# The 60 dependent steps that invert the 32 by 32 triangles: from VectorE to GpSimd

## The chip, the cores and the metric

One core of a Trainium2 chip runs the whole network. The time is device microseconds (us) of one execution. Engines are called as in the profile: PE is TensorE (matmuls), DVE is VectorE, ACT is ScalarE, POOL is GpSimd, SP issues the weight loads.

## The reference

Two layers on 256 frames of width 2048 in float32. Layer 0 mixes tokens by RWKV-7 (16 heads of 64) beside a Mamba-2 scan, layer 1 by chunked attention; each is followed by a SwiGLU feed-forward. What matters here is the RWKV-7 recurrence:

```
def step(S, inp):
    r_t, w_t, k_t, v_t, a_t, b_t = inp
    sa = jnp.einsum('bhvk,bhk->bhv', S, a_t)
    S = S * w_t[:, :, None, :] + sa[..., None] * b_t[:, :, None, :] + v_t[..., None] * k_t[:, :, None, :]
    return S, jnp.einsum('bhvk,bhk->bhv', S, r_t)
```

The kernel does it in four chunks of 64 frames. Within a chunk each step feeds on the ones before it, so that a unit triangular system of 64 rows is solved for each head: its inverse is built from two triangles of 32 rows on the diagonal and one block under them.

## The kernel before, in words

Every large product x W is a stream (`mm_chunk` and `stream`, lines 223 to 264): SP loads a weight tile, ACT makes its rounded part `hi` (line 240), DVE the rest `lo` (line 241, two inputs in SBUF), and PE multiplies hi and lo with both halves of the activations (lines 260 to 262). One weight tile of 128 by 512 makes six such matmuls of 512 columns, three for each half of the frames. `hi` and `lo` have five buffers each in layer 0's mixer, so DVE can be at most five tiles ahead of PE.

`mixer0` (line 393) handles the RWKV heads in two halves of eight (`rwkv_half`, line 481). A half projects k, r and v through the stream, and then:

- PE forms the products `aa` of all chunks and heads (line 576), and DVE masks them into `AA` (line 580).
- DVE transposes the two diagonal blocks of 32 chunk-head pairs into `NB` (line 589, two instructions).
- The forward substitution follows (lines 590 to 595): for i from 1 to 30 one multiplication writes `itmp`, and one addition puts it into the rows of `NB` that are left. Each of the 60 instructions reads what the one before it wrote. They work on 64 partitions and on (31 - i) x i elements of each, from 30 to 240; over i these are 4960 elements, so 9920 for both instructions.
- POOL sets the diagonal to one (line 596). DVE transposes the result into `Sf` (line 624, two instructions) and `TG` (line 625).
- PE needs `TG` for the 32 small matmuls `ga` (line 633), and `TG` and `Sf` for the 32 `gb` (line 640). With them the 64-row inverse is complete.
- The four chunks then go one after another (`cx`, `cu`, `ch`, `cy`, lines 651 to 717).

Beside this, PE runs `bo` (line 603) and the transpositions `bt` and `vt` (lines 612 and 616). After both halves comes the Mamba-2 part; for each of two groups it has transpositions `xt` (line 817), a mask `L` multiplied on POOL (line 826), cumulative sums `sg` (line 831), the exponential and a product on ACT and DVE, and `yd` (line 838).

The order in which instructions stand on each engine is set at build time by a scheduler that works with times of its own and with priorities: the stream has one raised by 4000, the rest of the mixer has none. On the chip every engine takes its instructions strictly in that order, so an instruction that waits holds up all that stand behind it on its engine. POOL otherwise has memsets (lines 596, 618, 621, 688), a few DMA issues and the four multiplications of line 826.

The line that the change touches is 146, and it acts on lines 593 and 595:

```
inv = dve
...
inv.tensor_tensor(tv, NB[:, i + 1:32, i:i + 1].broadcast_to([64, nt, i]),
                  NB[:, i:i + 1, 0:i].broadcast_to([64, nt, i]), op=ALU.mult)
inv.tensor_tensor(NB[:, i + 1:32, 0:i], NB[:, i + 1:32, 0:i], tv, op=ALU.add)
```

Of the kernel before, what the change touches and what calls it, by code (L numbers as in the profile page):

```python
# [142 lines left out]
def encoder_body(ctx: ExitStack, tc: tile.TileContext, A):  # L143
    nc = tc.nc
    act, dve, pool, pe = nc.scalar, nc.vector, nc.gpsimd, nc.tensor
    inv = dve

    cst = ctx.enter_context(tc.tile_pool(name="cst", bufs=1))
    wpool = ctx.enter_context(tc.tile_pool(name="wpool", bufs=5))
# [846 lines left out]
```

## Time and profile before

| | |
|---|---|
| median of three runs | 2382.67 us (2381.77 to 2384.16) |
| the profiled execution | 2384.66 us, its span 2382.8 us |
| busy in the span: PE, DVE, ACT, POOL | 2352.1, 1428.8, 1267.5, 32.4 us |
| mean granted PE clock | 0.992 |
| first chain of substitutions, on DVE | from 115.55 to 149.37 us |
| second chain | from 266.73 to 320.10 us |

Times in the trace count from the span's start. A matmul's end is modelled, so PE counts as busy in stretches where it is slow: what it gets done is seen from the distance between the starts of its matmuls, from its waits and from the granted clock (1.00 is 2.4 GHz, 0.50 is 1.2 GHz).

### The profile page before, as it was taken

Reading aid. Unit: us, or ns where it says so; the run is one execution under the profiler, and the core shown is the slowest. Engines: PE = TensorE matmul, PEld = TensorE weight load, DVE = VectorE, ACT = ScalarE, POOL = GpSimd, SP = SyncE. Lnnn points to the kernel's source line nnn. Section 1 sums busy time; section 2 is a strip of 40 time slices with the busy share of each in tenths; the row PEclk is TensorE's granted clock in tenths of the full one; section 3 lists DMA queues with packets and bytes.
Section 4 is the critical chain, followed back from the end, with each engine's and each line's share of the span. In section 5 each row is a group of like instructions: output and inputs, shape, how many; then the busy total and the mean of one; then the engine's idle time right before and its main releaser. Section 6 shows DMA issues by size and latency. Waiting matters only on the chain.

```text
span 2382.8 us, 31654 instructions
## 1 busy us (share of the span) xinstructions
PE 2352.1 (99%) x11426; PEld 1923.9 (81%) x11426; DVE 1428.8 (60%) x2380; ACT 1267.5 (53%) x2254; POOL 32.4 (1%) x61
## 2 busy tenths in 40 slices
PE   9999999999999999999999999999999999999998
PEld 7767777878888888888887888887888888888887
DVE  6876977765555555555557555557555555555554
ACT  6646545665545545544446555556555545454443
POOL 0000000000000000000000000000000000000000
PEclk9989999999999999999999999999999999999999
DMA  7434434666666666666665655565666666666664
GB/s 239 144 116 123 133 106 151 188 176 197 190 187 193 188 190 189 193 186 202 197 206 182 186 178 165 170 194 180 192 188 192 189 188 189 193 187 194 201 197 146
DMA packets 119357, 429.17 MB, mean 180 GB/s; under 512 B 13408, under 2 KB 13664, under 8 KB 119200
## 3 DMA queue, kind: packets, MB, share of 16 engines
q1 hardware_dynamic: 115280, 415.35, 57.2%
q0 software_dynamic: 2400, 9.18, 1.4%
q10 hardware_dynamic: 1520, 2.63, 0.4%
q8 instruction: 89, 1.46, 0.3%
q14 instruction: 68, 0.56, 0.1%
HBM read 425.01 MB, written 2.10 MB: 179 GB/s over the span
## 4 chain that ended last, share of the span: by engine, by line
PE 93%; DVE 4%; ACT 1%; DMA 1%; issue 1%; SPq 0%; DVEq 0%; ACTq 0%
PE mm_w_gu L260 13%; PE mm_w_gu L262 13%; PE mm_w_gu L261 13%; PE mm_w_dn L260 7%; PE mm_w_dn L262 7%; PE mm_w_dn L261 7%; PE mm_w_qkv L261 4%; PE mm_w_qkv L260 4%; PE mm_w_qkv L262 4%; PE mm_w_in L262 3%; PE mm_w_in L261 3%; PE mm_w_in L260 3%; PE mm_w_oab L260 1%; PE mm_w_oab L262 1%; PE mm_w_oc L262 1%; PE mm_w_oc L260 1%
## 5 line engine op out<-in xcount | busy, mean ns | idle before, releaser
L241 DVE TENSOR_TENSOR lo_w_gu<-raw_w_gu,hi_w_gu 128x512 fp32r<-128x512 f32 x704 | 485.8, 691 | 417.4 <-ACT hi_w_gu L240 414.9
L240 ACT CAST hi_w_gu<-raw_w_gu 128x512 fp32r<-128x512 f32 x704 | 438.4, 624 | 452.7 <-DVE lo_w_gu L241 404.9
L261 PE MATMUL mm_w_gu<-lo_w_gu,sh_f 128*128 128x512 f32 x1408 | 550.0, 391 | 0.0
L260 PE MATMUL mm_w_gu<-hi_w_gu,sh_f 128*128 128x512 f32 x1408 | 549.3, 390 | 0.6 <-ACT sh_f L299 0.5
L262 PE MATMUL mm_w_gu<-hi_w_gu,sl_f 128*128 128x512 f32 x1408 | 548.6, 390 | 0.0
L241 DVE TENSOR_TENSOR lo_w_dn<-raw_w_dn,hi_w_dn 128x512 fp32r<-128x512 f32 x352 | 242.8, 691 | 221.6 <-ACT hi_w_dn L240 221.0
L240 ACT CAST hi_w_dn<-raw_w_dn 128x512 fp32r<-128x512 f32 x352 | 219.0, 624 | 248.3 <-DVE lo_w_dn L241 238.6
L260 PEld LDWEIGHTS mm_w_gu<-hi_w_gu,sh_f 128*128 128x128 f32 x1408 | 264.3, 188 | 57.9 <-ACT sh_f L299 3.4
L262 PEld LDWEIGHTS mm_w_gu<-hi_w_gu,sl_f 128*128 128x128 f32 x1408 | 264.4, 188 | 55.5 <-DVE sl_f L300 1.2
L261 PEld LDWEIGHTS mm_w_gu<-lo_w_gu,sh_f 128*128 128x128 f32 x1408 | 264.4, 188 | 54.1 <-DVE lo_w_gu L241 0.3
L261 PE MATMUL mm_w_dn<-lo_w_dn,hh 128*128 128x512 f32 x704 | 274.1, 389 | 0.0
L262 PE MATMUL mm_w_dn<-hi_w_dn,hl 128*128 128x512 f32 x704 | 274.0, 389 | 0.0
L260 PE MATMUL mm_w_dn<-hi_w_dn,hh 128*128 128x512 f32 x704 | 273.9, 389 | 0.0
L241 DVE TENSOR_TENSOR lo_w_qkv<-raw_w_qkv,hi_w_qkv 128x512 fp32r<-128x512 f32 x192 | 132.2, 690 | 104.5 <-ACT hi_w_qkv L240 104.0
L240 ACT CAST hi_w_qkv<-raw_w_qkv 128x512 fp32r<-128x512 f32 x192 | 119.0, 621 | 110.3 <-DVE lo_w_qkv L241 64.8
L260 PE MATMUL mm_w_in<-hi_w_in,sh_in 128*128 128x512 f32 (+1 forms) x384 | 156.7, 408 | 1.7 <-ACT hi_w_in L240 1.7
L262 PE MATMUL mm_w_in<-hi_w_in,sl_in 128*128 128x512 f32 (+1 forms) x384 | 157.7, 411 | 0.0
L261 PE MATMUL mm_w_in<-lo_w_in,sh_in 128*128 128x512 f32 (+1 forms) x384 | 155.7, 405 | 0.0
L240 ACT CAST hi_w_in<-raw_w_in 128x512 fp32r<-128x512 f32 x184 | 112.3, 619 | 81.5 <-PE mm_w_in L262 71.5
L262 PEld LDWEIGHTS mm_w_dn<-hi_w_dn,hl 128*128 128x128 f32 x704 | 132.2, 188 | 27.6
L260 PEld LDWEIGHTS mm_w_dn<-hi_w_dn,hh 128*128 128x128 f32 x704 | 132.2, 188 | 27.3
L261 PEld LDWEIGHTS mm_w_dn<-lo_w_dn,hh 128*128 128x128 f32 x704 | 132.2, 188 | 27.2
(349 smaller groups left out, 2824.9 us busy)
## 6 DMA issues: line engine op xcount, KB each, us to landing
raw_w_gu<-in_w_gu SPq DMA_DIRECT2D x352, 512.0 KB, 3.6
raw_w_dn<-in_w_dn SPq DMA_DIRECT2D x176, 512.0 KB, 3.7
raw_w_qkv<-in_w_qkv SPq DMA_DIRECT2D x96, 512.0 KB, 3.6
raw_w_in<-in_w_in SPq DMA_DIRECT2D x92, 512.0 KB, 3.7
raw_w_oab<-in_w_oab SPq DMA_DIRECT2D x32, 512.0 KB, 4.2
raw_w_oc<-in_w_oc SPq DMA_DIRECT2D x32, 512.0 KB, 4.2
bias<-in_bias POOLq DMA_DIRECT2D x4, 768.0 KB, 6.6
x_in<-in_x SPq DMA_DIRECT2D x4, 512.0 KB, 9.0
```

The costliest lines, as they stand in the source:

```text
L240: act.copy(hi, raw[:, h, :])
L241: dve.tensor_tensor(lo, raw[:, h, :], hi.bitcast(F32), op=ALU.subtract)
L260: pe.matmul(o, lhsT=xh, rhs=h_[:, :width], start=k_ == 0, stop=False)
L261: pe.matmul(o, lhsT=xh, rhs=l_[:, :width], start=False, stop=False)
L262: pe.matmul(o, lhsT=xl, rhs=h_[:, :width], start=False, stop=k_ == nk - 1)
```

## The change

The 120 instructions of the two chains (60 in each half) are issued on POOL. All other lines stay as they are.

```
-    inv = dve
+    inv = pool
```

The scheduler builds another order from it. Three places matter; names end in buffer numbers, and "x2" means that the row is there twice in a row.

On POOL, where the first half's chain begins. Before:

```order
L598 DMA g_0_1255<-in_g 128x1024
L618 MEMSET uv_1266 64x512 x2
L618 MEMSET uv_1267 64x512 x2
L621 MEMSET Sf_1320 32x32x32
L596 MEMSET NB_986 64x32
```

With the change:

```order
L598 DMA g_0_1255<-in_g 128x1024
L593 ISA
L593 TENSOR_TENSOR itmp_988<-NB_986 64x30
L595 TENSOR_TENSOR NB_986<-NB_986,itmp_988 64x30
L593 TENSOR_TENSOR itmp_988<-NB_986 64x58
```

The chain stands ahead of the memsets of `uv` and `Sf`; in the second half four memsets of `uv` and the one of `Sf` stand within it. The row `ISA` stood ahead of line 826 before.

On DVE, what stands around the transpositions of the finished `NB` in the first half. Before:

```order
L595 TENSOR_TENSOR NB_986<-NB_986,itmp_988 64x30
L241 TENSOR_TENSOR lo_w_in_1_1_1956<-raw_w_in_1_1949,hi_w_in_1_1_1955 128x512
L624 STREAM_TRANSPOSE Sf_1320<-NB_986 32x32x32
L241 TENSOR_TENSOR lo_w_in_2_0_1974<-raw_w_in_2_1971,hi_w_in_2_0_1973 128x512
L624 STREAM_TRANSPOSE Sf_1320<-NB_986 32x32x32
L625 STREAM_TRANSPOSE TG_987<-NB_986 32x32x32
```

With the change:

```order
L604 TENSOR_TENSOR bv_1257<-bo_1258,bkv_468 128x512
L241 TENSOR_TENSOR lo_w_in_3_0_1733<-raw_w_in_3_1730,hi_w_in_3_0_1732 128x512
L604 TENSOR_TENSOR bv_1257<-bo_1261,bkv_468 128x512
L241 TENSOR_TENSOR lo_w_in_3_1_1737<-raw_w_in_3_1730,hi_w_in_3_1_1736 128x512
L625 STREAM_TRANSPOSE TG_987<-NB_986 32x32x32
L241 TENSOR_TENSOR lo_w_in_4_0_1755<-raw_w_in_4_1752,hi_w_in_4_0_1754 128x512
L624 STREAM_TRANSPOSE Sf_1320<-NB_986 32x32x32 x2
```

Between the second row of line 589 and the first of these transpositions stood 22 rows of line 241; now there are 10. In the second half there were 33 and are now 8; with the change line 624 comes first there, then two rows of line 241, line 624, one row of line 241, and line 625.

On PE, where the first half's `ga` stands among the stream. Before:

```order
L260 MATMUL mm_w_in_0_1925<-hi_w_in_1_0_1951,sh_in_122 128x512
L261 MATMUL mm_w_in_0_1925<-lo_w_in_1_0_1952,sh_in_122 128x512
L633 MATMUL ga_1325<-TG_987,AA_937 32x32 x32
L262 MATMUL mm_w_in_0_1925<-hi_w_in_1_0_1951,sl_in_123 128x512
```

With the change:

```order
L262 MATMUL mm_w_in_0_1662<-hi_w_in_2_0_1710,sl_in_125 128x512
L616 MATMUL vt_1313<-cc,bkv_468 128x128 x4
L633 MATMUL ga_1325<-TG_987,AA_937 32x32 x32
L260 MATMUL mm_w_in_1_1663<-hi_w_in_2_0_1710,sh_in_124 128x512
```

The stream matmuls (lines 260 to 262) counted in the whole order: from the last `aa` of the first half to its `ga` 160 before and 77 now; from there to the last `aa` of the second half 246 and 257; from there to the second half's `ga` 227 and 85. Eight transpositions of line 424 move behind `ga` in each half as well; those of the first half still stand ahead of the second half's `aa`. The first group's `xt`, `sg` and `yd` stood between the matmuls of the second half's four chunks; now they follow them, with runs of 7 and 9 stream matmuls between them.

## Rows read from the trace of the kernel before

**Rows 1.** The page: busy time by engine, and the chain that ended last.

```profile
PE 2352.1 (99%) x11426; PEld 1923.9 (81%) x11426; DVE 1428.8 (60%) x2380; ACT 1267.5 (53%) x2254; POOL 32.4 (1%) x61
...
PE 93%; DVE 4%; ACT 1%; DMA 1%; issue 1%; SPq 0%; DVEq 0%; ACTq 0%
```

**Rows 2.** Busy by stretch: us, PE, PEld, DVE, ACT, POOL; PE clock, DMA share, GB/s.

```profile
160.00:164.00 4.00, 4.00 (x69) 2.46 (x67) 0.69 (x1) 0.91 (x2) 0.00 (x0) 0.50 0.41 129
...
328.00:332.00 4.00, 4.00 (x73) 3.24 (x73) 2.86 (x5) 0.92 (x2) 0.00 (x0) 0.50 0.59 216
...
400.00:404.00 4.00, 3.13 (x14) 2.25 (x12) 1.65 (x3) 0.57 (x2) 0.00 (x0) 1.00 0.75 249
404.00:408.00 4.00, 1.59 (x8) 1.59 (x8) 3.56 (x5) 2.57 (x6) 0.00 (x0) 0.79 0.45 143
408.00:412.00 4.00, 4.00 (x13) 2.97 (x13) 0.84 (x2) 0.07 (x1) 1.83 (x1) 0.50 0.43 133
```

**Rows 3.** PE in order of time: start, us, work, [idle before it, what ended it].

```profile
121.06 0.82 PE L424 MATMUL tr<-cc,tm 128*128 128x128 f32 x6
134.28 0.63 PE L612 MATMUL bt<-cc,bkv 128*128 128x128 f32 x4 [1.71 <-DVE bv L604]
146.96 0.39 PE L260 MATMUL mm_w_in<-hi_w_in,sh_in 128*128 128x512 f32 x1
...
149.68 0.39 PE L260 MATMUL mm_w_in<-hi_w_in,sh_in 128*128 128x512 f32 x1
...
156.55 0.74 PE L633 MATMUL ga<-TG,AA 32*32 32x32 f32 x64 [2.44 <-DVE TG L625]
...
327.94 1.07 PE L633 MATMUL ga<-TG,AA 32*32 32x32 f32 x64 [3.93 <-DVE TG L625]
```

**Rows 4.** DVE in order of time: `NB` in the halves, and line 567.

```profile
98.94 1.67 DVE L567 SCALAR_TENSOR_TENSOR r<-r,pf,a 128x256 f32<-128x256 f32 x4
112.28 2.03 DVE L589 STREAM_TRANSPOSE NB<-AA 32x1024 f32<-32x1024 f32 x1
...
262.07 4.02 DVE L589 STREAM_TRANSPOSE NB<-AA 32x1024 f32<-32x1024 f32 x2
```

**Rows 5.** DVE groups by line and shape: busy us, mean ns of one.

```profile
L241 DVE TENSOR_TENSOR lo_w_in<-raw_w_in,hi_w_in 128x512 fp32r<-128x512 f32 x184 | 124.7, 687 | 35.1 <-ACT hi_w_in L240 34.3
L531 DVE TENSOR_TENSOR lw<-c,lw 128x1024 f32<-128x1024 f32 x2 | 2.4, 1222 | 0.0
L593 DVE TENSOR_TENSOR itmp<-NB 64x240 f32<-64x240 f32 x4 | 1.6, 391 | 0.0
L593 DVE TENSOR_TENSOR itmp<-NB 64x30 f32<-64x30 f32 x4 | 0.7, 184 | 0.0
```

**Rows 6.** POOL in order of time, from the start to line 826.

```profile
0.75 0.31 POOL L173 MEMSET warm<- 128x256 f32 x1 [0.29 <-POOLq L988]
...
15.17 0.18 POOL L193 COPY tick<-x_in 128x1 f32<-128x1 f32 x1 [12.81 <-DMA x_in<-in_x]
...
66.72 0.54 POOL L598 DMA_DIRECT2D g<-in_g  x1 [49.25 <-PE lo L520]
...
100.72 0.98 POOL L618 MEMSET uv<- 64x512 f32 x2 [8.37 <-DVE r L567]
...
275.67 0.94 POOL L621 MEMSET Sf<- 32x1024 f32 x1 [21.39 <-DVE NB L595]
316.28 0.15 POOL L596 MEMSET NB<- 64x32 f32 x1 [39.67 <-DVE NB L595]
316.45 2.14 POOL L826 TENSOR_TENSOR L<-cc,adt 128x1024 f32<-128x1024 f32 x1
334.15 1.90 POOL L826 TENSOR_TENSOR L<-cc,adt 128x1024 f32<-128x1024 f32 x1 [15.56 <-PE xt L817]
```

**Rows 7.** DVE in order of time, beside POOL's line 826.

```profile
316.75 1.91 DVE L593 TENSOR_TENSOR itmp<-NB 64x58 f32<-64x58 f32 x1
318.59 0.46 DVE L768 SCALAR_TENSOR_TENSOR xf<-tr_cv,hcv,xf 128x253 f32<-128x253 f32 x1
```

## The prediction

> **What bounds the kernel now.** I read the page first. PE is busy for 99% of the span and makes up 93% of the chain that ended last; POOL is almost idle [rows 1]. The stream therefore sets the time, and the change can only win where PE waits or runs slowly, and only lose by making PE wait. I looked next at PE in order of time for the two places where it needs the inverted triangles. Twelve stream matmuls start between 146.96 and 149.68, so one costs 0.227 us. PE then waits 2.44 us for `TG` before the first `ga`, at 156.55, and 3.93 us before the second, at 327.94 [rows 3]. By stretch, both waits are followed by some us at a granted clock of 0.50, half speed [rows 2]. That is all there is to win at these places: 6.4 us of waiting, and at least 2 us for each of the two stretches of 4 us at half clock.
>
> Last I looked at what hides the chain now. It shares DVE with the `lo` instructions, but PE has long work ahead of `ga`: 160 stream matmuls in the first half and 227 in the second, counted in the order of instructions. So a chain on DVE of 34 and 53 us costs PE almost nothing.
>
> **The chain itself.** On DVE one instruction takes 184 ns for 30 elements and 391 ns for 240 [rows 5]: 0.986 ns an element and 154 ns fixed. A half's 60 instructions with 9920 elements thus cost DVE 60 x 0.154 + 9.8 = 19.0 us, which DVE now saves twice. It gains PE nothing of its own where DVE waits for PE anyway.
>
> On POOL only line 826 is of this kind. It takes 1.90 us for 1024 elements undisturbed; a copy of one element takes 0.18 us [rows 6]. That gives 1.68 ns an element. The chain of a half then costs 60 x 0.18 = 10.8 us and 9920 x 1.68 ns = 16.7 us: 27.5 us.
>
> Each of the 60 instructions also needs the result of the one before. No row shows POOL waiting for itself. At the lower end the hand-over is free. The nearest row is POOL's start at 100.72 [rows 6], 0.11 us after line 567 ended on DVE at 98.94 + 1.67 = 100.61 [rows 4]. At the upper end I put 0.29 us, POOL's idle time ahead of `warm` [rows 6]. I take 0.11, since it is a wait for data on POOL: 6.6 us a half.
>
> DVE and POOL also get in each other's way. While line 826 ran on POOL from 316.45, a DVE instruction of line 593 with 58 elements and two inputs in SBUF took 1.91 us, and it ended with POOL's; the next on DVE, line 768, which reads PSUM and SBUF, had its usual length [rows 7]. The `lo` instructions of 687 ns [rows 5] have two inputs in SBUF, and 10 stand ahead of line 625 in the first half, 8 ahead of line 624 in the second. After that DVE itself waits for the chain and disturbs it no more. A `lo` costs the chain between nothing and 0.69 us; I take 0.4, somewhat over half: 4.0 and 3.2 us.
>
> The Trainium skill, SBUF — State Buffer, section "Who interferes with whom", says that a DVE instruction with two SBUF inputs and a GpSimd instruction that reads SBUF shut each other out for a whole instruction; the trace agrees, with the 1.91 us above.
>
> So the first chain takes T = 27.5 + 6.6 + 4.0 = 38.1 us. The second has five memsets among its instructions, four of `uv` (0.98 us for two) and one of `Sf` (0.94) [rows 6]: T' = 27.5 + 6.6 + 3.2 + 2.9 = 40.2 us. The row `ISA` is free: it stood between 316.28 + 0.15 and 316.45 before, and POOL now meets it after 67.3, long before the chain [rows 6].
>
> The Trainium skill, GPSIMD Engine Reference, section "Performance versus the Vector engine", speaks against the change: an addition of two inputs takes GpSimd 1.96 times as long as DVE. Line 531 on DVE takes 1.22 us for 1024 elements [rows 5], so the rows here give 1.56. By the page's ratio the 27.5 us would be an estimated 37.2, and the time below would come out near 2445.
>
> **What becomes late.** The scheduler has put `ga` where it believes the chain to be over: 77 stream matmuls after the last `aa` instead of 160, and 85 instead of 227. If the chain ends later, PE waits in front of `ga`, and DVE waits in front of line 625 or 624 with all `lo` behind it, so the stream can't fill the hole. In the first half PE could be at `ga` by about 135: the transpositions end at 121.9, 27 stream matmuls (6.1 us) and eight groups of `bt` and `vt` of 0.63 us [rows 3] make 133, and `bt` waits some 2 us for line 604. With `NB` ready at 114.3 [rows 4] a chain of over 20 us is late.
>
> The sum follows the two `ga`:
>
> - First `ga`: 114.3 + T + 2.0 (line 625; a transposition takes 2.03 [rows 4]) = 154.4 instead of 156.55: T - 40.2 = -2.1 us. PE arrives about as before but has done 83 stream matmuls less.
> - From there to the second half's `aa`: 257 stream matmuls instead of 246, and eight transpositions more (0.82 us for six [rows 3]): 2.5 + 1.1 = +3.6 us.
> - Second `ga`: `NB` is ready at 266.1 [rows 4]. Behind the chain come line 624 twice, line 625 and three `lo`, 8.2 us. Relative to `NB` this is T' + 8.2 instead of 61.8: T' - 53.6 = -13.4 us.
> - What is then still to do: 83 - 11 + 142 = 214 stream matmuls, 48.5 us, and eight transpositions, 1.1 us: +49.6 us.
>
> Together T + T' - 40.6 = 37.7 us. One term is left: the first Mamba group's `xt`, `sg` and `yd` were woven into the second half's chunks and now stand with short runs of stream, as the second group's do. There PE loses 0.87 + 2.41 us between 400 and 408, and about 2 us at half clock after that [rows 2]; with the 0.79 in between 5.6 us. Lower end nothing, upper end twice that with a longer half clock, 12 us. I take 5.6.
>
> The profiled execution took 2384.66 us. 2384.7 + 37.7 + 5.6 = 2428.0; the median of the runs lies 2.0 lower, so **2426 us**.
>
> **The rivals.**
>
> - *A dear hand-over.* At 0.29 us, and with every `lo` costing 0.69, T = 51.8 and T' = 53.3: +64.5, with 12 for the rest 2459 us. For it: 120 hand-overs in a row, whose price no row shows. Against: the 0.11 us.
> - *A short chain that is still late.* No hand-over, no mutual blocking: T = 27.5, T' = 30.4, +17.3 and nothing else: 2400 us. For it: POOL's memsets follow each other without a gap; against: those don't depend on each other.
> - *Faster: POOL keeps DVE's pace.* If both chains are over when PE comes to `ga`, PE loses both waits and the half clock behind them, 6.4 + 4 = 10.4 us: 2372 us. It decides at T = 20. For it: DVE needs only 19.0 for the same work; against: 1.90 us on POOL for what takes DVE 1.22.
> - *No change*, when the chains are late by as much as the waits that were there, T + T' near 40 us: 2383. Nothing in the rows gives such a T.
> - That the chain does not move is excluded: all 120 rows of lines 593 and 595 stand on POOL.
>
> **How the numbers follow.** The forecast, T from 33 to 45 us, has 0.62; the dear hand-over 0.20; the short chain 0.10; no change 0.04; faster 0.04. The range takes in the first three with their bounds, from 2400 to 2459 us. A measurement of this kernel can tell about 0.2% from no change, 4.8 us. Slower has 0.92, same 0.04, faster 0.04.
>
> **What would show it.** The steps are right if lines 593 and 595 on POOL start 0.6 to 0.7 us apart on the mean, if the first `ga` stands near 154 us and waits some 20 us for `TG`, if DVE shows one idle time of that kind ahead of line 625 and one ahead of line 624, and if single `lo` instructions beside the chain take over 0.8 us. The prediction is wrong if PE reaches `ga` without a wait, or if the loss lies elsewhere than in front of the two `ga`.

## Result and profile after

The changed kernel takes 2421.29 us, median of 5 runs (2420.92 to 2424.2), beside 2383.56 us for the kernel before, run next to it: a ratio of 1.0164, 95% interval 1.015 to 1.0177. The change costs 37.7 us. The profiled execution took 2424.2 us, its span is 2422.4 us.

The page, first busy time by engine and then the chain that ended last:

```profile
PE 2352.7 (97%) x11426; PEld 1921.5 (79%) x11426; DVE 1399.2 (58%) x2260; ACT 1268.1 (52%) x2254; POOL 98.2 (4%) x181
...
PE 91%; POOL 3%; issue 3%; DVE 2%; ACT 1%; DMA 0%; SPq 0%; DVEq 0%; POOLq 0%; ACTq 0%
```

PE is busy as long as before [rows 1], 2352.7 against 2352.1 us, in a span that is 39.6 us longer: PE stands still more. POOL, absent from that chain before, now has 3% of it, for the two inversions. DVE has 29.6 us less to do, and that bought nothing.

POOL in order of time (start, us, work, the idle time before it and what ended it): the beginning of the first chain, some instructions beside a `lo` (122.93 and 125.64) and some without one, its last one, and the first and last of the second chain.

```profile
112.85 0.74 POOL L593 TENSOR_TENSOR itmp<-NB 64x30 f32<-64x30 f32 x1 [47.12 <-DVE NB L589]
...
122.32 0.53 POOL L593 TENSOR_TENSOR itmp<-NB 64x184 f32<-64x184 f32 x1
122.93 0.91 POOL L595 TENSOR_TENSOR NB<-NB,itmp 64x184 f32<-64x184 f32 x1
...
125.64 1.12 POOL L593 TENSOR_TENSOR itmp<-NB 64x210 f32<-64x210 f32 x1
...
149.31 0.32 POOL L593 TENSOR_TENSOR itmp<-NB 64x84 f32<-64x84 f32 x1
149.71 0.36 POOL L595 TENSOR_TENSOR NB<-NB,itmp 64x84 f32<-64x84 f32 x1
...
151.53 0.24 POOL L595 TENSOR_TENSOR NB<-NB,itmp 64x30 f32<-64x30 f32 x1
...
263.12 0.24 POOL L593 TENSOR_TENSOR itmp<-NB 64x30 f32<-64x30 f32 x1 [45.65 <-DVE NB L589]
...
302.35 0.24 POOL L595 TENSOR_TENSOR NB<-NB,itmp 64x30 f32<-64x30 f32 x1
```

From 112.77, when `NB` was ready, to 151.77 the first chain took 39.0 us; from 263.03 to 302.59 the second took 39.6. Between one instruction and the next lie 0.08 us (149.31 + 0.32 = 149.63, next start 149.71). On the mean they start 0.66 us apart in the first chain ((151.53 - 112.85) / 59).

DVE in order of time, where it hands `NB` over, two `lo` beside the chain, and where it takes the triangles back:

```profile
110.74 2.02 DVE L589 STREAM_TRANSPOSE NB<-AA 32x1024 f32<-32x1024 f32 x1
...
122.47 0.93 DVE L241 TENSOR_TENSOR lo_w_in<-raw_w_in,hi_w_in 128x512 fp32r<-128x512 f32 x1 [0.16 <-ACT hi_w_in L240]
...
125.64 0.67 DVE L241 TENSOR_TENSOR lo_w_in<-raw_w_in,hi_w_in 128x512 fp32r<-128x512 f32 x1
...
151.80 2.00 DVE L625 STREAM_TRANSPOSE TG<-NB 32x1024 f32<-32x1024 f32 x1 [25.49 <-POOL NB L595]
...
261.02 2.01 DVE L589 STREAM_TRANSPOSE NB<-AA 32x1024 f32<-32x1024 f32 x1
...
302.63 1.90 DVE L624 STREAM_TRANSPOSE Sf<-NB 32x1024 f32<-32x1024 f32 x1 [23.53 <-POOL NB L595]
```

PE in order of time, at the same places:

```profile
153.95 1.08 PE L633 MATMUL ga<-TG,AA 32*32 32x32 f32 x64 [23.05 <-DVE TG L625]
...
305.10 0.79 PE L261 MATMUL mm_w_in<-lo_w_in,sh_in 128*128 128x512 f32 x1 [20.36 <-DVE lo_w_in L241]
...
310.35 1.08 PE L633 MATMUL ga<-TG,AA 32*32 32x32 f32 x64 [4.03 <-DVE TG L625]
```

DVE stands for 25.5 and 23.5 us in front of lines 625 and 624, with the `lo` queued behind them, and PE for 23.05 us in front of the first `ga` and 20.36 + 4.03 us around the second; before these were 2.44 and 3.93 us [rows 3]. The new waiting is 41.1 us. By stretch (columns as in [rows 2]):

```profile
120.00:140.00 20.00, 10.90 (x62) 8.17 (x60) 5.58 (x13) 8.75 (x16) 17.86 (x28) 0.84 0.23 73
140.00:160.00 20.00, 6.05 (x76) 4.95 (x77) 7.63 (x7) 1.39 (x3) 12.53 (x29) 0.50 0.00 1
280.00:300.00 20.00, 4.74 (x21) 3.58 (x20) 0.00 (x0) 2.49 (x4) 17.84 (x32) 0.68 0.03 12
300.00:320.00 20.00, 10.87 (x157) 6.93 (x157) 11.02 (x13) 2.47 (x6) 2.19 (x8) 0.50 0.26 79
```

While POOL works on the later part of a chain, PE, DVE, ACT and even the DMAs stop: 1 GB/s between 140 and 160. The granted clock falls to 0.50 in each hole. It stays there for some us behind each `ga`, as it did before. Those stretches, first in the kernel before, then with the change:

```profile
157.20:170.80 13.60, 13.60 (x114) 8.53 (x106) 4.07 (x8) 4.72 (x9) 0.00 (x0) 0.50 0.26 80
327.90:334.60 6.70, 6.66 (x83) 5.10 (x84) 4.47 (x7) 2.11 (x4) 0.45 (x1) 0.50 0.36 133
```

```profile
154.00:160.70 6.70, 6.70 (x77) 5.02 (x77) 6.11 (x7) 1.60 (x3) 0.16 (x1) 0.50 0.12 28
310.40:324.60 14.20, 14.20 (x167) 9.75 (x168) 4.69 (x9) 5.42 (x10) 0.00 (x0) 0.50 0.31 94
```

Together they are 20.3 us before and 20.9 now. So the clock behind the holes does not explain the loss; the waiting does.

### The profile page after: what moved, and what is told of

Its sections match the earlier page's. It is cut to its first block, busy times and chain, and to the rows that moved or that the text cites. A ratio compares the mean times of both kernels' runs of the same rounds, so it can differ in the third digit from the quotient of the medians.

```text
span 2422.4 us, 31663 instructions
## 1 busy us (share of the span) xinstructions
PE 2352.7 (97%) x11426; PEld 1921.5 (79%) x11426; DVE 1399.2 (58%) x2260; ACT 1268.1 (52%) x2254; POOL 98.2 (4%) x181
## 4 chain that ended last, share of the span: by engine, by line
PE 91%; POOL 3%; issue 3%; DVE 2%; ACT 1%; DMA 0%; SPq 0%; DVEq 0%; POOLq 0%; ACTq 0%
PE mm_w_gu L260 13%; PE mm_w_gu L261 13%; PE mm_w_gu L262 13%; PE mm_w_dn L261 7%; PE mm_w_dn L262 7%; PE mm_w_dn L260 7%; PE mm_w_qkv L260 4%; PE mm_w_qkv L262 4%; PE mm_w_qkv L261 4%; PE mm_w_in L262 3%; PE mm_w_in L261 3%; PE mm_w_in L260 3%; POOL itmp L593 1%; POOL NB L595 1%; PE mm_w_oc L262 1%
## 5 line engine op out<-in xcount | busy, mean ns | idle before, releaser
L241 DVE TENSOR_TENSOR lo_w_in<-raw_w_in,hi_w_in 128x512 fp32r<-128x512 f32 x184 | 124.9, 690 | 51.5 <-ACT hi_w_in L240 50.9
L260 PEld LDWEIGHTS mm_w_dn<-hi_w_dn,hh 128*128 128x128 f32 x704 | 132.2, 188 | 27.5
```

The costliest lines, as they stand in the source:

```text
L241: dve.tensor_tensor(lo, raw[:, h, :], hi.bitcast(F32), op=ALU.subtract)
L260: pe.matmul(o, lhsT=xh, rhs=h_[:, :width], start=k_ == 0, stop=False)
```

## Experiments

Two theories stood against each other. **A**: PE's loss is the time by which a chain ends after PE has nothing else left, because DVE, the consumer of the chain, stops with the `lo` behind it. **R1**: POOL's work costs wherever it stands, by shutting DVE out. The kernel before, run beside each group, took 2383.0 to 2383.5 us.

### One half alone: e1_first_half

```diff
                         for i in range(1, 31):
+                            inv = pool if hf == 0 else dve
```

> The chain of the first half alone on POOL, the second half's on DVE. Theory A: each half's chain costs on its own what PE and DVE stand still in front of it, about 18 us each: 2398 to 2406 us, with one stop of some 20 us. A loss from one common cause (code loading, the clock, Mamba's order) would give nearly all of the 38 us or nearly none.

Measured: 2399.87 us, ratio 1.0071 (1.0057 to 1.0085), +16.9 us. PE in order of time, at the first `ga`:

```profile
154.99 1.08 PE L634 MATMUL ga<-TG,AA 32*32 32x32 f32 x64 [22.99 <-DVE TG L626]
```

As expected: one stop, and somewhat under half of the 37.7 us; 20.8 us are left for the second half, which was not run alone.

### The same order, shorter chains: e15_half_chain and e16_two_thirds

```diff
-                        for i in range(1, 31):
+                        for i in range(1, (16, 31)[hf]):
                             inv = pool if hf == 0 else dve
```

and 23 in place of 16 in e16_two_thirds. Steps 16 to 30 (23 to 30) of the first half's chain are not computed.

> e1_first_half with the steps i = 16 to 30 of the first half's chain left out (they are not computed at all); the order of the instructions on PE and DVE is that of e1_first_half, so only the chain's length differs. In e1_first_half step 15 ended 17.3 us ahead of the last step, and PE waited 23.0 us in front of ga. Theory A (each us that the chain ends after PE's arrival costs one): a wait of 5.7 us, 2380 to 2385 us. Rival (work on POOL costs by the clock, by blocking DVE or by its mere presence): well over 2388 us.

> As the run before, with the steps i = 23 to 30 of the first half's chain left out. Step 22 ended 7.8 us ahead of the last in e1_first_half. Theory A: a wait of 15.2 us, 2390 to 2395 us, on a line with e1_first_half (2399.9) and e15_half_chain.

Measured: 2382.78 us, ratio 0.9999 (0.999 to 1.0008), and 2392.75 us, ratio 1.0037 (1.0025 to 1.005). The first `ga` of the one and of the other:

```profile
137.60 1.07 PE L634 MATMUL ga<-TG,AA 32*32 32x32 f32 x64 [5.95 <-DVE TG L626]
```

```profile
147.71 1.08 PE L634 MATMUL ga<-TG,AA 32*32 32x32 f32 x64 [15.45 <-DVE TG L626]
```

Together with e1_first_half, in three kernels with one order on PE, DVE and ACT: chains of 21.6, 31.1 and 38.9 us (from the first start to the last end), waits of 5.95, 15.45 and 22.99 us, times of 2382.8, 2392.8 and 2399.9 us. From the shortest to the longest, 17.3 us of chain are 17.0 us of waiting and 17.1 us of time. So each us by which the chain outlasts PE's arrival costs one, as theory A has it. Between these three, work on POOL has no price beyond its length: 30 instructions more there add 17.0 us of waiting and nothing else.

### PE's order alone: e3_late, e3b_later, and e4_late_dve as the control

In e3_late the next chunks of the stream are written ahead of the consumers, so that PE has more to do before `ga`:

```diff
...
+                for n in ((4,), (7, 8))[hf]:
+                    ahead[n] = mm_chunk("w_in", n, st)
                 for q in range(2):
                     p0 = 32 * q
                     dve.transpose(Sf[p0:p0 + 32, :, p0:p0 + 32].rearrange("p b t -> p t b"), NB[p0:p0 + 32])
```

`proj` takes what lies in `ahead`. In e3b_later chunk 7 goes through `proj` there and chunks 8 and 9 stand ahead. e4_late_dve is e3_late with `inv = dve`; the scheduler then puts the two `ga` behind 160 and 172 stream matmuls instead of 146 and 132, so it is a control for the way of writing, not for the exact order.

> The chain stays on POOL, but the stream of chunk 4 (first half) and of chunks 7 and 8 (second half) is written ahead of its consumers, so that in the order of instructions 146 and 132 stream matmuls stand between the last aa and ga instead of 77 and 85. Theory A (the loss is that the consumers stand too early for a chain of 39 us): PE reaches ga about 3 us and 5 to 10 us before the triangles are there, and nearly the whole loss is gone, 2380 to 2396 us. Rival R1 (POOL itself costs, by shutting DVE out and by slow hand-overs): the chain still takes 39 us and the time stays at 2410 to 2424 us.

> As the run before, with chunk 7 taken out of PSUM and chunk 9 written ahead too, so that 228 stream matmuls stand ahead of the second ga. Theory A: no wait of more than 4 us is left at either ga, 2374 to 2390 us. R1: 2410 us or more.

> The kernel before, chain on DVE, written in the order of e3_late (160 and 172 stream matmuls ahead of ga). Theory A: the order decides and the engine hardly does, so within 12 us of e3_late: 2376 to 2392 us. R1: about 2384 us here and some 35 us more in e3_late.

Measured: e3_late 2409.28 us, ratio 1.0109 (1.0095 to 1.0123); e3b_later 2427.54, ratio 1.0186 (1.0173 to 1.02); e4_late_dve 2384.48, ratio 1.0 (0.999 to 1.001). Theory A missed all three as it was put here: e4_late_dve lies in its range, but 24.8 us from e3_late and not within 12. R1's numbers came nearer: 2409.28 is 0.7 us under its range, e3b_later and e4_late_dve are where it had them, and 24.8 us stand between the two engines where it had some 35. The waits of e3_late, first PE's, then DVE's from 100 to 420 us (us in total, times, longest):

```profile
PE mm_w_in L263 <- DVE lo_w_in L243: 38.1, 2, 19.6
```

```profile
DVE TG L633 <- POOL NB L599: 25.5, 1, 25.5
DVE Sf L632 <- POOL NB L599: 22.8, 1, 22.8
```

The edit gives back 12 of the 37.7 us. It moved `ga` on PE, but DVE's order hardly: 10 `lo` still stood between `NB` and the first transposition of each half. DVE stopped for 25.5 and 22.8 us as before, and PE now starved in the middle of its stream, waiting for `lo`. For what is left, the queue that decides is DVE's, not PE's. e3b_later has the same stops on DVE (25.5 and 22.8 us) and loses 18 us more in Mamba's stage, where PE waits 5.4 us at `xt` and 4.0 at `yd`, for the reason that e14_later_tg_first shows below.

### DVE's order too: e8_queue and e9_queue_dve

```diff
+                if hf == 1:
+                    early[7] = proj(7)
+                for n, cut in (((4, 0), (5, 4)), ((8, 0), (9, 8)))[hf]:
+                    ahead[n] = mm_part("w_in", n, st, cut or 16)
+                    next(ahead[n])
+                with tc.issue_after(los[(83, 151)[hf]].ins):
...
```

`mm_part` is `mm_chunk` that can stop after `cut` of its 16 steps, `los` holds the instructions of line 241, and below the `with` stand the three transpositions. e9_queue_dve is the same with `inv = dve`.

> The chain stays on POOL. Now DVE's consumers themselves (lines 624 and 625 of the change) are queued late, behind 23 and 23 to 25 lo instructions after NB instead of 10 and 8 to 10, by an order edge to a lo, and 170 and 164 stream matmuls stand ahead of the two ga. Theory A, narrowed after e3_late (the loss is that DVE stops in front of lines 624 and 625 with the lo instructions behind them, so that PE's order alone mends nothing): no stop of more than 4 us in front of a lo or a ga is left, 2376 to 2396 us. Rival R1 (work beside POOL's costs what e5_shadow lost, 19 us): 2400 to 2412 us.

> The same order as e8_queue with the chain on DVE. Theory A: within 8 us of e8_queue, 2376 to 2392 us. R1: 2384 us, and e8_queue 16 us or more above it.

Measured: e8_queue 2401.85 us, ratio 1.0078 (1.0065 to 1.009); e9_queue_dve 2384.41, ratio 1.0003 (0.9994 to 1.0012). Queueing DVE's consumers later gives back half of the loss. Yet theory A missed e8_queue's 2376 to 2396 us and the 8 us between the two, and R1 met both of its numbers: 2400 to 2412 us, and 16 us or more between the engines. e8_queue, PE at the two `ga`:

```profile
163.85 1.08 PE L657 MATMUL ga<-TG,AA 32*32 32x32 f32 x64 [11.42 <-DVE TG L649]
...
327.19 1.07 PE L657 MATMUL ga<-TG,AA 32*32 32x32 f32 x64 [11.62 <-DVE TG L649]
```

and the first chain on POOL, first and last instruction:

```profile
113.25 0.74 POOL L611 TENSOR_TENSOR itmp<-NB 64x30 f32<-64x30 f32 x1 [47.12 <-DVE NB L607]
...
156.43 0.24 POOL L613 TENSOR_TENSOR NB<-NB,itmp 64x30 f32<-64x30 f32 x1
```

In e9_queue_dve, DVE from `NB` to the first transposition behind the chain:

```profile
111.25 2.03 DVE L607 STREAM_TRANSPOSE NB<-AA 32x1024 f32<-32x1024 f32 x1
...
148.88 2.03 DVE L648 STREAM_TRANSPOSE Sf<-NB 32x1024 f32<-32x1024 f32 x1
```

With nearly the same order (both `ga` stand behind the same stream matmuls), the chain lasts 113.25 to 156.67, 43.4 us, on POOL, and at most 113.28 to 148.88, 35.6 us, on DVE, although DVE does all the `lo` in between. With 12 more `lo` beside it POOL's chain is 4.5 us longer than in the change (43.4 against 38.9, from the first start to the last end). PE waits 23.0 us at the two `ga` instead of 4.8 in e9_queue_dve: 18.2 us, and the times differ by 17.4. So each theory has a part of it: the loss is PE's waiting for a late chain, as in A, and the chain is longer on POOL, in part because of the blocking that R1 names.

### Later still: e14_later_tg_first

The edit of e8_queue, with chunks 4, half of 5, 7, 8, 9 and a quarter of 10 ahead, and `TG` transposed before the two `Sf`.

> As e8_queue (chain on POOL), with the consumers queued later still, behind 26 and 29 lo instructions after NB, 194 and 204 stream matmuls ahead of the two ga, and with TG transposed ahead of the two Sf. Theory A: e8_queue's 23 us of waiting in front of the two ga go, and with them its whole loss: 2378 to 2392 us. Rival (the stream is used up: what stands beside the chain is missing later, in Mamba's stage, or POOL's work hurts DVE by itself): 2395 to 2405 us, with the idle time of PE after 350 us or in front of other instructions.

Measured: 2412.15 us, ratio 1.0126 (1.011 to 1.0142): the rival's side, and beyond it. PE's waits, and two stretches of Mamba's stage:

```profile
PE gb L665 <- DVE TG L661: 10.1, 2, 5.5
PE xt L842 <- DVE xf L804: 9.2, 1, 9.2
...
PE ga L658 <- DVE TG L646: 3.2, 2, 2.4
```

```profile
400.00:420.00 20.00, 14.25 (x73) 11.42 (x72) 14.71 (x27) 8.80 (x16) 0.00 (x0) 0.92 0.84 285
420.00:440.00 20.00, 12.01 (x46) 9.78 (x46) 8.85 (x10) 4.01 (x6) 4.06 (x2) 0.50 0.01 3
```

The waits at `ga` are down to 3.2 us. But `gb` waits 10.1 us, since both `Sf` now stand on DVE between `TG` and its second half, and Mamba's second group has lost its filler: between 400 and 440 us PE is busy for 26.3 of 40 us, and the clock is 0.50 in the second half of that. Counted in the order of instructions, the projection has 1152 stream matmuls, and in e14_later_tg_first and e3b_later all of them stand ahead of that group's `xt`, `sg` and `yd`. In the kernel before, the group begins behind the 1096th and the rest is spread between its steps. The stream is a fixed stock: what is spent beside a chain is missing later. Whether another order hides 43 us on POOL without a loss elsewhere stays open; the orders tried here do not.

### Two more: e6_split and e5_shadow

```diff
                         for i in range(1, 31):
+                            inv = pool if i < 16 else dve
```

> Steps i = 1 to 15 of the chain on POOL and 16 to 30 on DVE, so that a chain lasts some 20 us on POOL and some 12 to 16 on DVE among the lo instructions. Theory A with the prediction's point (a chain hurts by as much as it ends after PE comes to ga, and the scheduler puts ga at 108 stream matmuls after the last aa here instead of 77): 2386 to 2400 us. If any step on POOL cost the same wherever it stands, half of the loss: 2402 us.

Measured: 2402.51 us, ratio 1.0084 (1.007 to 1.0098). A's number was missed and the other one met, but not for its reason, since the same 15 steps cost nothing in e15_half_chain's first half. The waits of DVE show why (100 to 460 us):

```profile
DVE itmp L594 <- POOL NB L596: 26.1, 2, 14.9
```

DVE's half of the chain waits for POOL's, 26.1 us in all, again with the `lo` behind it, and PE waits 15.0 us for `lo`. Theory A counted the end of the chain only; a hand-over to DVE anywhere in its queue stops the stream.

e5_shadow keeps the chain on DVE and lets POOL do work of the same shapes for nobody:

```diff
...
+                            pool.tensor_tensor(sv, sh_in[:, i + 1:32, i:i + 1].broadcast_to([64, nt, i]),
+                                               sh_in[:, i:i + 1, 0:i].broadcast_to([64, nt, i]), op=ALU.mult)
+                            pool.tensor_tensor(sv, sh_in[:, i + 1:32, 0:i], sv, op=ALU.add)
```

with `sh_in` a part of `AA`, `sv` a part of the scratch tile, and the memset of line 596 on DVE.

> The kernel before, chain on DVE, and beside it on POOL 60 instructions a half of the chain's shapes, on a scratch tile that nobody reads; the memset of the diagonal goes to DVE. It measures only what POOL's work does to its neighbours. Theory A: 2380 to 2392 us. R1: DVE's chain and the lo instructions are held up by some 10 to 20 us a half, 2404 to 2424 us.

Measured: 2402.66 us, ratio 1.0081 (1.0068 to 1.0093). Here A's 2380 to 2392 us were far off, and R1's 2404 to 2424 were missed by 1.3 us: R1 came much nearer. Groups of DVE between 100 and 330 us (busy us, mean ns):

```profile
L241 DVE TENSOR_TENSOR lo_w_in<-raw_w_in,hi_w_in 128x512 fp32r<-128x512 f32 x94 | 68.1, 733 | 18.8 <-ACT hi_w_in L240 18.5
...
L594 DVE TENSOR_TENSOR itmp<-NB 64x240 f32<-64x240 f32 x4 | 2.0, 510 | 0.0
...
L594 DVE TENSOR_TENSOR itmp<-NB 64x30 f32<-64x30 f32 x3 | 1.1, 380 | 0.0
```

Beside POOL's work the chain's instructions on DVE take 380 instead of 184 ns for 30 elements and 510 instead of 391 for 240, and a `lo` 733 instead of 687 [rows 5]. From `NB` to the first transposition behind the chain DVE needs 47.2 us in the first half, where it needed 35.6 before (114.31 to 149.90), and before the first `ga` PE waits for what DVE makes late: 3.6 us for `bv` and 4.1 us for a `hi`, since ACT had stood 10.2 us behind line 509 on DVE:

```profile
131.47 0.47 ACT L504 ACTIVATE bkv<-tr,om 128x256 f32<-128x256 f32 x1 [10.21 <-DVE bkv L509]
```

So mutual blocking is dear where both engines run long rows of small instructions. In the change DVE has mostly `lo` there, 10 and 8 of them.

### `TG` first, with the chain on DVE: e12_dve_tg_first

```diff
+                tg = dve.transpose(TG[0:32].rearrange("p b i -> p i b"), NB[0:32].rearrange("p t i -> p i t"))
+                with tc.issue_after(tg.ins):
...
-                dve.transpose(TG[0:32].rearrange("p b i -> p i b"), NB[0:32].rearrange("p t i -> p i t"))
```

> The kernel before, chain on DVE, with line 625 (TG) ahead of the two of line 624 (Sf) on DVE, so that ga starts some 4 us sooner. The two waits of 2.4 and 3.9 us in front of ga go: 2376 to 2381 us. If PE's waits there are worth nothing, 2383 us.

Measured: 2378.19 us, ratio 0.9981 (0.9973 to 0.9989) to the kernel before: 5.3 us faster. The chain stays on DVE; `ga` needs `TG` alone and no longer waits for two transpositions that only later work needs. PE's waits:

```profile
PE ga L634 <- DVE TG L622: 3.1, 2, 2.3
...
PE gb L641 <- DVE TG L637: 1.6, 2, 1.4
...
PE cu L675 <- DVE Sf L644: 1.5, 1, 1.5
```

Of 6.4 us of waiting at `ga` 3.1 are left, but 1.6 and 1.5 us of it have moved on to `gb` and `cu`, so the waits do not make the gain. What differs is the clock: the stretch that was at 0.50 behind the first `ga` is at full clock here.

```profile
157.20:170.80 13.60, 13.60 (x197) 9.36 (x198) 5.29 (x10) 6.14 (x12) 0.00 (x0) 1.00 0.33 113
```

At half clock those 13.6 us had done 6.8 us of work. The mean granted clock is 0.994 to 0.997 in all runs of this kernel, and 0.992 to 0.994 in those of the kernel before beside them, but for one of 2373.38 us at 0.997. PE stood for 0.84 us in front of that `ga` here and for 2.44 before [rows 3]; that the shorter wait is what kept the clock up was not tested by itself. The first `ga` starts 37.8 us after `NB` (150.63 after 112.79) instead of 42.2 (156.55 [rows 3] after 114.31).

## Why the prediction was right

The sum came out at +43.3 us for the profiled execution and at 2426 us; measured were +39.5 (2424.2 against 2384.66) and 2421.3. The mechanism is the one that was forecast, a late chain with DVE and PE standing in front of its result; some of its terms are right by luck. The steps:

- **The chain.** T was put at 38.1 us and is 39.0; T' at 40.2 and is 39.6. By terms, in the first half: the undisturbed rows (0.23 us for 30 elements, 0.61 to 0.69 for 240) give 29.1 us for 60 instructions instead of 27.5 (the smaller row of each size, summed). The hand-over is 0.08 us, not 0.11, 4.8 us for 60. All 60 together ran for 34.0 us; the 4.9 us above 29.1 stand where 4.0 were put for the blocking by 10 `lo`. It fell mostly on POOL's side: single instructions took up to 1.12 us there, but only 3 of the 18 `lo` beside the chains took over 0.8 us, 0.93 in the first half. The starts were 0.66 us apart, as the forecast had it.
- The Trainium skill, SBUF — State Buffer, section "Who interferes with whom", calls the port pair that DVE and GpSimd share an exclusive lock and has the order of issue decide who blocks. The trace agrees: the `lo` of 122.47 began while POOL's instruction of 122.32 to 122.85 ran, and took 0.93 us; POOL's next one began at 122.93, while that `lo` ran, and took 0.91 us, with its end 0.44 us after the end of the `lo`.
- The Trainium skill, GPSIMD Engine Reference, section "Performance versus the Vector engine", has an addition of two inputs at 1.96 times DVE's time, for 2048 elements. Here line 595 takes 0.64 us undisturbed for 240 elements on POOL (at 133.79), and 0.391 on DVE in the kernel before: 1.64 times. The measurement decides; the estimate of 2445 us by the page's ratio was too high.

```profile
L595 DVE TENSOR_TENSOR NB<-NB,itmp 64x240 f32<-64x240 f32 x4 | 1.6, 391 | 0.0
```

```profile
133.79 0.64 POOL L595 TENSOR_TENSOR NB<-NB,itmp 64x240 f32<-64x240 f32 x1
```

- **First `ga`**: 154.4 us predicted, 153.95 measured. Two errors cancel in part: `NB` was ready 1.5 us earlier than the 114.3 taken from the kernel before, and the chain was 0.9 us longer.
- **From there to the second `NB`**: +3.6 us predicted, but the distance is 109.08 us (263.03 less 153.95) where it was 109.54 (266.09 less 156.55): -0.5. This step failed in size. It counted the 11 matmuls and 8 transpositions more, but took the half clock behind the first `ga` as unchanged. That stretch was 13.6 us and is now 6.7, since the clock fell within the hole already: about 3.4 of the 4.1 us.
- **Second `ga`**: T' + 8.2 = 48.4 us after `NB` predicted, 47.3 measured (310.35 less 263.03), with the order of transpositions and `lo` as counted.
- **What is then still to do**: +49.6 us, and +5.6 for Mamba, predicted; the rest of the span is 2112.05 us instead of 2054.86, +57.2. That this fits is luck in part, for the Mamba term failed. PE's waits behind the second `ga`, up to the end of this projection, before and with the change:

```profile
PE yd L838 <- DVE L L833: 3.3, 1, 3.3
```

```profile
PE yd L838 <- DVE L L833: 1.9, 2, 1.3
PE sg L831 <- POOL L L826: 1.5, 2, 0.9
PE xt L817 <- DVE xf L779: 0.2, 1, 0.2
```

  They are 3.6 us instead of 3.3, and half clock in Mamba's stage lasts 3.4 us (396.3 to 399.7) instead of 6.8 (406.3 to 413.2): no loss there, where 5.6 us were put. In its place the half clock behind the second `ga` lasts 14.2 us instead of 6.7, which costs some 3.8 us more and cancels the gain behind the first. The rest of the 57.2 us was not taken apart.
- **Where the wait stands.** 20 us were foretold in front of the first `ga`; it is 23.05. In the second half the wait stands mostly at a stream matmul that wants a `lo`, 20.36 us, and only 4.03 at `ga` itself. The cause is the stop of DVE that was predicted, but PE met it two instructions earlier than it said.

Of the rivals, the dear hand-over fell with 0.08 us, and the short chain with T = 39. The faster case had its point at T = 20. But PE was ready for the first `ga` at 130.9 (153.95 less 23.05), not at 135, and e15_half_chain still waits 5.95 us at T = 21.7, counted from `NB`: the point without any wait lies nearer 16 us there. Its price was too small as well: the half clock behind the two `ga`, put at 4 us together, cost 10.2 (half of 20.3). At T = 21.7 the first half is even with the kernel before.

## What to carry to other kernels

Work moved to an idle engine takes its latency along: what matters is when its consumer, in order on a busy engine, reaches the front of that engine's queue, and what is queued behind it. Moving the bottleneck engine's own order mends little (12 of 37.7 us in e3_late) while the consumer's queue stops its feeders. Filler spent beside a long chain is missing elsewhere, so first look for consumers that can go ahead of others, as `TG` here. And a gain or loss at a wait can lie in the clock behind it: read both.

## What the runs showed of the hardware

Dependent instructions follow each other on POOL with 0.08 us between them, less than the 0.11 and 0.29 us seen before [rows 4, 6]. Work on POOL that nobody waits for cost this kernel 19.4 us (2402.66 less the 2383.31 us of the kernel before beside it), while DVE's small instructions of 184 ns took 380. And a chain that DVE carried among its `lo` in 35.6 us took POOL, which had little else to do, 39.0 us beside 10 `lo` and 43.4 beside 22.
